# A macaron hybrid layer in fp32: the FFN's hidden activations transposed on VectorE in 32x32 blocks instead of on TensorE

## The chip, the cores and the metric

One core of a Trainium2 chip runs the whole layer. The metric is device time in microseconds of one execution, median of several runs. Engine names follow the profile: PE is TensorE's matmul, PEld its weight load, DVE is VectorE, ACT is ScalarE, POOL is GpSimd, SP is SyncE.

## The reference

One decoder layer on x of 256 rows by 2048 columns, all in float32: a half-step of SwiGLU FFN, a mixer with three groups of attention heads, and a second half-step of SwiGLU FFN. The change touches the two FFNs alone.

```python
def rms_norm(x, g):
    xf = x.astype(jnp.float32)
    y = xf * lax.rsqrt(jnp.mean(xf * xf, axis=-1, keepdims=True) + EPS)
    return (y * g.astype(jnp.float32)).astype(x.dtype)

def swiglu(x, w_gate, w_up, w_down):
    return (jax.nn.silu(x @ w_gate) * (x @ w_up)) @ w_down
...
        x = x + 0.5 * swiglu(rms_norm(x, ffn1_norm[l]), ffn1_gate[l], ffn1_up[l], ffn1_down[l])
        ...                                # the mixer: three groups of heads, then w_out
        x = x + 0.5 * swiglu(rms_norm(x, ffn2_norm[l]), ffn2_gate[l], ffn2_up[l], ffn2_down[l])
```

The gate and up weights are 2048 x 5632, the down weights 5632 x 2048.

## The kernel before

Every projection multiplies in three terms. A weight tile is split into a rounded part `hi` (ScalarE, L203) and the rest `lo` (VectorE, L204); the activations are split the same way (`split`, L207 to L209), and `mm_rows` (L241 to L248) adds hi times hi, hi times lo and lo times hi into one PSUM accumulator. The activations stand on the PE as weights of 128x128, and 512 columns of the layer's weights stream past them. `load_w` brings 256 rows by 512 columns at a time; I call this a block. It feeds 12 matmuls: two k tiles, two row tiles t, three terms. The raw tile has four buffers, `hi` and `lo` have three each, so the `hi` of a block can be written only when the PE has finished the block three before it.

`ffn` (L267) runs 11 rounds j of 512 hidden columns. A round is a gate projection (8 blocks, L292), SiLU on ScalarE into `g` (L298), an up projection (8 blocks, L300), and the product on VectorE (L302), which leaves h as 256 rows on partitions. The down projection needs h with hidden columns on partitions. So `transpose_h` (L273) has the PE transpose eight 128x128 squares into PSUM (L280), and splits them from there into the two halves of `hT` (L285, two calls of 512 elements per partition on each of ScalarE and VectorE). After the rounds, four down projections of 22 blocks each (L314 on) read `hT`.

What runs beside the projections is cut into stages by generators. `lanes.tick()` after each block (L263) advances them by one stage; `lanes.put` queues a task for one of two lanes that each own a PSUM buffer, `lanes.run` starts one without a lane. The engine order is then set by the framework's scheduler when the program is built. Within an engine, the order is fixed.

At the end of the last down projection (c = 3 of the second FFN), VectorE adds each row tile to x (L316), and `store` (L694) sends each as 128 x 512 to the output, t = 0 by SP's queue and t = 1 by ACT's.

Of the kernel before, what the change touches and what calls it, by code (L numbers as in the profile page):

```python
# [8 lines left out]
F32 = mybir.dt.float32  # L9
# [7 lines left out]
P = 128  # L17
D = 2048
NK = D // P
SEQ = 256  # L20
NT = SEQ // P
DFF = 5632
NF = DFF // P
# [3 lines left out]
KB = 2  # L27
# [53 lines left out]
def hybrid_layer(ctx, tc, x, mem, ffn1_norm, ffn1_gate, ffn1_up, ffn1_down, mix_norm, mem_norm,  # L81
# [3 lines left out]
    nc = tc.nc  # L85

    x, mem, out = x[0], mem[0], out[0]
    gate1, up1, down1 = ffn1_gate[0], ffn1_up[0], ffn1_down[0]
    gate2, up2, down2 = ffn2_gate[0], ffn2_up[0], ffn2_down[0]
# [11 lines left out]
    def psum(tag, name):  # L101

        return ps.tile([P, 2, 512], F32, tag=tag, bufs=2 if tag == "acc" else 1, name=name)

    lanes = Lanes()


    x_sb = cpool.tile([P, NT, D], F32, name="x_sb")
# [4 lines left out]
    for k0, nk in XCUT:  # L113
        cols = slice(k0 * P, (k0 + nk) * P)
        (nc.scalar if k0 else nc.sync).dma_start(x_sb[:, :, cols], xv[:, :, cols])

    ident = cpool.tile([P, P], F32, name="ident")
# [78 lines left out]
    def load_w(w, k0, nk, c0, width, name):  # L196
        raw = wpool.tile([P, KB, 512], F32, tag="raw", bufs=4, name=f"raw_{name}")
        hi = wpool.tile([P, KB, 512], F32R, tag="hi", bufs=3, name=f"hi_{name}")
        lo = wpool.tile([P, KB, 512], F32R, tag="lo", bufs=3, name=f"lo_{name}")
        r, h, l = (t[:, :nk, :width] for t in (raw, hi, lo))  # L200
        nc.sync.dma_start(
            r, w[k0 * P:(k0 + nk) * P, c0:c0 + width].rearrange("(k p) c -> p k c", p=P))
        nc.scalar.copy(h, r)  # L203
        nc.vector.tensor_tensor(out=l, in0=r, in1=h.bitcast(F32), op=ALU.subtract)  # L204
        return h, l

    def split(dst_hi, dst_lo, src):  # L207
        nc.scalar.copy(dst_hi, src)
        nc.vector.tensor_tensor(out=dst_lo, in0=src, in1=dst_hi.bitcast(F32), op=ALU.subtract)  # L209

    def transpose_chunk(xT, src, k0, nk, g0, name, pause=1):
# [16 lines left out]
            yield 1  # L228
        return stages

    def square_sums(ss, src, c):
        for t in range(NT):
            junk = small.tile([P, 512], F32, tag="junk", bufs=2, name="junk")
            nc.scalar.activation(junk, src[:, t, :], AF.Square, accum_out=ss[:, t, c:c + 1])
# [6 lines left out]
    def mm_rows(acc, aT, kt, wh, wl, first, last):  # L241

        w = wh.shape[-1]
        for t in range(NT):
            hi, lo = aT[:, kt, 0, t * P:(t + 1) * P], aT[:, kt, 1, t * P:(t + 1) * P]
            nc.tensor.matmul(acc[:, t, :w], hi, wh, start=first, stop=False)  # L246
            nc.tensor.matmul(acc[:, t, :w], hi, wl, start=False, stop=False)  # L247
            nc.tensor.matmul(acc[:, t, :w], lo, wh, start=False, stop=last)  # L248

    def project(acc, aT, w, c0, width, kts, nk_all, done, name, before=None):  # L250

        for k0, n in kts:
            k = k0
            while k < k0 + n:
                b = min(KB, k0 + n - k)
                if before:
                    before(k)
                wh, wl = load_w(w, k, b, c0, width, f"{name}_{k}")
                for j in range(b):
                    mm_rows(acc, aT, k + j, wh[:, j, :], wl[:, j, :], done == 0, done == nk_all - 1)  # L260
                    done += 1
                k += b
                lanes.tick()  # L263
        return done


    def ffn(xT, before, stats, wg, wu, wd, after, name):  # L267

        with tc.tile_pool(name=f"h_{name}", bufs=1, reuse_waits="tile") as hpool, \
                tc.tile_pool(name=f"ht_{name}", bufs=2, reuse_waits="tile") as htmp:  # L270
            hT = hpool.tile([P, NF, 2, SEQ], F32R, name=f"hT_{name}")

            def transpose_h(j, h):  # L273

                def stages(tag):
                    tp = psum(tag, f"th_{name}{j}")
                    tv = tp.rearrange("p a b -> p (a b)").rearrange("p (k s) -> p k s", k=4)
                    for k in range(4):
                        for t in range(NT):
                            nc.tensor.transpose(tv[:, k, t * P:(t + 1) * P], h[:, t, k * P:(k + 1) * P],  # L280
                                                ident)
                    yield 1
                    for b in range(2):
                        f = slice(4 * j + 2 * b, 4 * j + 2 * b + 2)
                        split(hT[:, f, 0, :], hT[:, f, 1, :], tv[:, 2 * b:2 * b + 2, :])  # L285
                    yield 1
                return stages

            rstd = None
            for j in range(DFF // 512):  # L290
                acc = psum("acc", f"g{name}{j}")
                project(acc, xT, wg, j * 512, 512, [(0, NK)], NK, 0, f"{name}g{j}",  # L292
                        None if j else before)
                if j == 0:
                    rstd = stats()
                g = htmp.tile([P, NT, 512], F32, tag="g", bufs=3, name=f"gs{name}{j}")
                for t in range(NT):
                    nc.scalar.activation(g[:, t, :], acc[:, t, :], AF.Silu, scale=rstd[:, t:t + 1])  # L298
                acc = psum("acc", f"u{name}{j}")
                project(acc, xT, wu, j * 512, 512, [(0, NK)], NK, 0, f"{name}u{j}")  # L300
                for t in range(NT):
                    nc.vector.scalar_tensor_tensor(out=g[:, t, :], in0=acc[:, t, :],  # L302
                                                   scalar=rstd[:, t:t + 1], in1=g[:, t, :],
                                                   op0=ALU.mult, op1=ALU.mult)
                lanes.put(f"hT{name}{j}", transpose_h(j, g))

            def before_d(k):
                if k >= NF - 4:
                    lanes.finish(f"hT{name}{DFF // 512 - 1}")

            for c in range(4):
                acc = psum("acc", f"d{name}{c}")
                project(acc, hT, wd, c * 512, 512, [(0, NF)], NF, 0, f"{name}d{c}", None if c else before_d)
                for t in range(NT):  # L314
                    xc = x_sb[:, t, c * 512:(c + 1) * 512]
                    nc.vector.scalar_tensor_tensor(out=xc, in0=acc[:, t, :], scalar=0.5, in1=xc,  # L316
                                                   op0=ALU.mult, op1=ALU.add)
                    after(c, t)

    def xchunk(c):  # L320
        return x_sb[:, :, c * 512:(c + 1) * 512]
# [6 lines left out]
    x0T = r1.tile([P, NK, 2, SEQ], F32R, tag="r1", name="x0T")  # L328
# [25 lines left out]
    def mem_stages_T(c):  # L354
        def stages(tag):
            raw = mem_raw(c)
            yield 3
            yield from transpose_chunk(lambda: memTs[0], lambda: raw, 4 * c, 4, G_MEM, f"mem{c}")(tag)
            square_sums(ssm, raw, c)
        return stages  # L360

    def after1(c, t):
        if t == 0:
            return
        if c == 0:
            memTs.append(r1.tile([P, NK, 2, SEQ], F32R, tag="r1", name="memT"))
        if c < 2:
            for i in (2 * c, 2 * c + 1):
                lanes.put(f"memT{i}", mem_stages_T(i), ("consts",))
        square_sums(ss1, xchunk(c), c)  # L370
# [2 lines left out]
        lanes.finish(*(f"ss0_{c}" for c in range(4)))  # L373
        return row_rstd(ss0, "x0")

    ffn(x0T, before0, stats0, gate1, up1, down1, after1, "a")
    memT = memTs[0]
    lanes.finish("memT3")

# [1 line left out]
    with tc.tile_pool(name="mix", bufs=1, reuse_waits="tile") as mx, \  # L381
# [39 lines left out]
        acc = psum("acc", "mk")  # L421
        project(acc, memT, w_mem_k, 0, 512, [(0, NK)], NK, 0, "mk")
        lanes.run("mk", heads_T(acc, 4, rm, 5, mkT, "mk"))
        acc = psum("acc", "mv")
# [8 lines left out]
        sv = slots[:, 30:32, :]  # L433
# [195 lines left out]
        acc = chunk(MEM_Q, 512, "mq")  # L629
# [4 lines left out]
        acc = chunk(FOX_F, 390, "sqa")  # L634
        for t in range(NT):
            nc.vector.scalar_tensor_tensor(out=z[:, t, :], in0=acc[:, t, 0:6], scalar=r1s[:, t:t + 1],
                                           in1=bias6, op0=ALU.mult, op1=ALU.add)
# [3 lines left out]
        acc = chunk(SWA_K, 512, "skv")  # L641
# [3 lines left out]
        acc = chunk(SWA_Q + 384, 384, "sqb")  # L645
# [4 lines left out]
        for half, (a, b) in (("a", (0, 3)), ("b", (3, 6))):  # L650
            for g, (c0, dst) in enumerate(((FOX_Q, fqT), (FOX_K, fkT))):
                name = f"f{'qk'[g]}{half}"
                acc = chunk(c0 + a * HD, 384, name)
# [6 lines left out]
        for half, a in (("a", 0), ("b", 384)):  # L660
            acc = chunk(FOX_V + a, 384, f"fv{half}")
# [14 lines left out]
        x2T = r1.tile([P, NK, 2, SEQ], F32R, tag="r1", name="x2T")  # L676
        for c in range(4):
            if c < 2:
                acc = accs[c]
                project(acc, mixT, w_out, c * 512, 512, late, 16, done[c], f"wo{c}l")  # L680
            else:
                acc = psum("acc", f"wo{c}")
                project(acc, mixT, w_out, c * 512, 512, [(0, 16)], 16, 0, f"wo{c}")
            xc = xchunk(c)
# [6 lines left out]

    ov = out.rearrange("(t p) d -> p t d", p=P)

    def store(c, t):  # L694
        cols = slice(c * 512, (c + 1) * 512)
        (nc.sync, nc.scalar)[t].dma_start(ov[:, t, cols], x_sb[:, t, cols])

    def stats2():
        lanes.finish("ss2_3")
        return row_rstd(ss2, "x2")  # L700

    ffn(x2T, lambda k: lanes.finish("bT3") if k == 12 else None, stats2, gate2, up2, down2, store, "b")


# [29 lines left out]
```

## Time and profile before

| what | value |
|---|---|
| median of 3 runs (lowest to highest) | 1833.58 us (1833.07 to 1834.23) |
| the profiled execution's own time | 1832.94 us |
| its span, first to last instruction | 1831.2 us |
| granted TensorE clock | 1.00 over the whole run |
| PE busy | 1818.1 us, 99% |
| DVE busy | 941.8 us, 51% |
| ACT busy | 846.1 us, 46% |
| the 88 transposes of h on PE in each FFN (L280) | 11.4 us busy |

Busy time counts an instruction from its start to its end. Instructions of one engine can overlap, so what one costs on the path is the distance from its start to the start of the next, which the timeline shows. Span and execution time differ by 1.7 us, which lies outside the instructions.

### The profile page before, as it was taken

How to read it: one execution, taken by the hardware profiler on the slowest of the kernel's cores; microseconds unless marked ns; L12 is line 12 of the kernel's file. 1: busy time of each engine (PE TensorE's matmuls, PEld its weight loads, DVE VectorE, ACT ScalarE, POOL GpSimd, SP SyncE). 2: the span in 40 equal slices, each digit the busy share in tenths (PEclk: the TensorE clock that was granted, in tenths of full speed). 3: DMA queues.
4: the chain of work that ended last, by engine and by line, in shares of the span. 5: the costliest groups of instructions: out<-in, count | busy, mean ns of one | idle time of the engine just before them, and what ended most of it. 6: DMA issues, size and time to landing. Idle time of an engine off the chain costs nothing.

```text
span 1831.2 us, 21875 instructions
## 1 busy us (share of the span) xinstructions
PE 1818.1 (99%) x8424; PEld 1532.2 (84%) x8424; DVE 941.8 (51%) x1127; ACT 846.1 (46%) x1148; POOL 11.6 (1%) x31
## 2 busy tenths in 40 slices
PE   8999999999999999999999999999999999999998
PEld 6888888888888888888999888888888888888887
DVE  5454545455545554645666455455545454544443
ACT  6444444444445444557666454444444444433332
POOL 2000000000000000000000000000000000000000
PEclk9999999999999999999999999999999999999999
DMA  7666666666666566565666556666666666666663
GB/s 235 191 190 189 190 190 188 192 189 190 190 190 206 188 216 193 167 178 156 181 156 183 171 185 193 186 193 188 192 184 190 189 189 190 191 193 203 205 207 127
DMA packets 182696, 344.55 MB, mean 188 GB/s; under 512 B 11130, under 2 KB 28096, under 8 KB 182464
## 3 DMA queue, kind: packets, MB, share of 16 engines
q1 hardware_dynamic: 180368, 339.04, 62.0%
q10 hardware_dynamic: 1696, 2.89, 0.5%
q8 instruction: 66, 1.08, 0.3%
q0 software_dynamic: 528, 1.22, 0.2%
q14 instruction: 38, 0.31, 0.0%
HBM read 341.01 MB, written 2.11 MB: 187 GB/s over the span
## 4 chain that ended last, share of the span: by engine, by line
PE 99%; DMA 0%; ACT 0%; DVE 0%; issue 0%; DVEq 0%; ACTq 0%
PE ga L246 4%; PE ga L248 4%; PE ga L247 4%; PE ua L246 4%; PE da L248 4%; PE gb L248 4%; PE db L248 4%; PE gb L247 4%; PE gb L246 4%; PE da L247 4%; PE ub L247 4%; PE ua L248 4%; PE da L246 4%; PE ua L247 4%; PE ub L248 4%; PE ub L246 4%
## 5 line engine op out<-in xcount | busy, mean ns | idle before, releaser
L204 DVE TENSOR_TENSOR lo_bu<-raw_bu,hi_bu 128x1024 fp32r<-128x1024 f32 x88 | 107.8, 1226 | 131.5 <-ACT hi_bu L203 131.5
L204 DVE TENSOR_TENSOR lo_au<-raw_au,hi_au 128x1024 fp32r<-128x1024 f32 x88 | 107.8, 1225 | 130.0 <-ACT hi_au L203 130.0
L204 DVE TENSOR_TENSOR lo_bd<-raw_bd,hi_bd 128x1024 fp32r<-128x1024 f32 x88 | 107.8, 1225 | 123.9 <-ACT hi_bd L203 123.9
L204 DVE TENSOR_TENSOR lo_ad<-raw_ad,hi_ad 128x1024 fp32r<-128x1024 f32 x88 | 107.8, 1225 | 116.7 <-ACT hi_ad L203 116.7
L203 ACT CAST hi_bd<-raw_bd 128x1024 fp32r<-128x1024 f32 x88 | 92.8, 1055 | 145.0 <-PE db L248 139.8
L204 DVE TENSOR_TENSOR lo_ag<-raw_ag,hi_ag 128x1024 fp32r<-128x1024 f32 x88 | 107.9, 1226 | 99.2 <-ACT hi_ag L203 99.2
L204 DVE TENSOR_TENSOR lo_bg<-raw_bg,hi_bg 128x1024 fp32r<-128x1024 f32 x88 | 107.7, 1224 | 99.1 <-ACT hi_bg L203 99.1
L203 ACT CAST hi_ad<-raw_ad 128x1024 fp32r<-128x1024 f32 x88 | 92.7, 1053 | 129.1 <-PE da L248 104.7
L203 ACT CAST hi_bg<-raw_bg 128x1024 fp32r<-128x1024 f32 x88 | 92.7, 1054 | 127.2 <-PE gb L248 68.3
L203 ACT CAST hi_ag<-raw_ag 128x1024 fp32r<-128x1024 f32 x88 | 92.8, 1054 | 121.3 <-PE ga L248 66.7
L203 ACT CAST hi_bu<-raw_bu 128x1024 fp32r<-128x1024 f32 x88 | 92.7, 1054 | 115.5 <-PE ub L248 79.0
L203 ACT CAST hi_au<-raw_au 128x1024 fp32r<-128x1024 f32 x88 | 92.7, 1054 | 115.3 <-PE ua L248 79.4
L246 PE MATMUL ga<-hi_ag,x0T 128*128 128x512 f32 x352 | 138.5, 393 | 0.0
L246 PE MATMUL gb<-hi_bg,x2T 128*128 128x512 f32 x352 | 137.9, 392 | 0.0
L246 PE MATMUL da<-hi_ad,hT_a 128*128 128x512 f32 x352 | 137.4, 390 | 0.0
L248 PE MATMUL ga<-hi_ag,x0T 128*128 128x512 f32 x352 | 137.4, 390 | 0.0
L247 PE MATMUL ga<-lo_ag,x0T 128*128 128x512 f32 x352 | 137.2, 390 | 0.0
L248 PE MATMUL gb<-hi_bg,x2T 128*128 128x512 f32 x352 | 137.1, 389 | 0.0
L247 PE MATMUL da<-lo_ad,hT_a 128*128 128x512 f32 x352 | 137.0, 389 | 0.0
L246 PE MATMUL ua<-hi_au,x0T 128*128 128x512 f32 x352 | 137.0, 389 | 0.0
L246 PE MATMUL db<-hi_bd,hT_b 128*128 128x512 f32 x352 | 137.0, 389 | 0.0
L248 PE MATMUL da<-hi_ad,hT_a 128*128 128x512 f32 x352 | 137.0, 389 | 0.0
(459 smaller groups left out, 3948.3 us busy)
## 6 DMA issues: line engine op xcount, KB each, us to landing
raw_ag<-in_ffn_gate_dram SPq DMA_DIRECT2D x88, 512.0 KB, 4.5
raw_au<-in_ffn_up_dram SPq DMA_DIRECT2D x88, 512.0 KB, 3.7
raw_ad<-in_ffn_down_dram SPq DMA_DIRECT2D x88, 512.0 KB, 4.1
raw_bg<-in_ffn_gate_dram SPq DMA_DIRECT2D x88, 512.0 KB, 4.2
raw_bu<-in_ffn_up_dram SPq DMA_DIRECT2D x88, 512.0 KB, 3.7
raw_bd<-in_ffn_down_dram SPq DMA_DIRECT2D x88, 512.0 KB, 4.4
raw_wo<-in_w_out_dram SPq DMA_DIRECT2D x16, 512.0 KB, 3.7
raw_mk<-in_w_mem_k_dram SPq DMA_DIRECT2D x8, 512.0 KB, 3.7
```

The source lines that it names most:

```text
L203: nc.scalar.copy(h, r)
L204: nc.vector.tensor_tensor(out=l, in0=r, in1=h.bitcast(F32), op=ALU.subtract)
L246: nc.tensor.matmul(acc[:, t, :w], hi, wh, start=first, stop=False)
L247: nc.tensor.matmul(acc[:, t, :w], hi, wl, start=False, stop=False)
L248: nc.tensor.matmul(acc[:, t, :w], lo, wh, start=False, stop=last)
```

## The change

`quad_transposes` is new: VectorE transposes 32x32 blocks. An instruction reads 32 partitions (group a of four) and writes 32 partitions (group b), eight blocks at a time, which are 256 elements per partition. Sixteen of them turn the 256 x 512 tile `g` into `raw`, 128 partitions by 4 by 256 in SBUF. They come in four stages of four. Then two stages split `raw` into `hT`. The task no longer needs a lane's PSUM buffer, and goes by `lanes.run`. `g` has two buffers instead of three, `raw` has one.

The end of the last down projection is reordered as well: `project_end` takes the last block apart, so that all six matmuls of t = 0 come before the six of t = 1. The second row tile is then added and stored in two halves of 256 columns.

```diff
+    def quad_transposes(dst, src):
+        sv = src.rearrange("p t (k b s) -> p b t k s", b=4, s=32)
+        dv = dst.rearrange("p k (t a s) -> p a t k s", t=NT, s=32)
+        for a in range(4):
+            for b in range(4):
+                nc.vector.transpose(out=dv[32 * b:32 * b + 32, a], in_=sv[32 * a:32 * a + 32, b])
+            yield 1
...
+    def project_end(acc, aT, w, c0, k0, n, name, landed):
+        tiles = []
+        for k in range(k0, k0 + n, KB):
+            wh, wl = load_w(w, k, KB, c0, 512, f"{name}_{k}")
+            tiles += [(wh[:, j, :], wl[:, j, :]) for j in range(KB)]
+        for t in range(NT):
+            for j, (wh, wl) in enumerate(tiles):
+                hi, lo = (aT[:, k0 + j, i, t * P:(t + 1) * P] for i in range(2))
+                nc.tensor.matmul(acc[:, t, :], hi, wh, start=False, stop=False)
+                nc.tensor.matmul(acc[:, t, :], hi, wl, start=False, stop=False)
+                nc.tensor.matmul(acc[:, t, :], lo, wh, start=False, stop=j == n - 1)
+            for c, width in ((0, 256), (256, 256)) if t else ((0, 512),):
+                landed(t, c, width)
+        lanes.tick()
...
             def transpose_h(j, h):
-                def stages(tag):
-                    tp = psum(tag, f"th_{name}{j}")
-                    tv = tp.rearrange("p a b -> p (a b)").rearrange("p (k s) -> p k s", k=4)
-                    for k in range(4):
-                        for t in range(NT):
-                            nc.tensor.transpose(tv[:, k, t * P:(t + 1) * P], h[:, t, k * P:(k + 1) * P],
-                                                ident)
+                raw = htmp.tile([P, 4, SEQ], F32, tag="raw", bufs=1, name=f"hr_{name}{j}")
+                yield from quad_transposes(raw, h)
+                for b in range(2):
+                    f = slice(4 * j + 2 * b, 4 * j + 2 * b + 2)
+                    split(hT[:, f, 0, :], hT[:, f, 1, :], raw[:, 2 * b:2 * b + 2, :])
                     yield 1
-                    for b in range(2):
-                        f = slice(4 * j + 2 * b, 4 * j + 2 * b + 2)
-                        split(hT[:, f, 0, :], hT[:, f, 1, :], tv[:, 2 * b:2 * b + 2, :])
-                    yield 1
-                return stages
...
-                g = htmp.tile([P, NT, 512], F32, tag="g", bufs=3, name=f"gs{name}{j}")
+                g = htmp.tile([P, NT, 512], F32, tag="g", bufs=2, name=f"gs{name}{j}")
...
-                lanes.put(f"hT{name}{j}", transpose_h(j, g))
+                lanes.run(f"hT{name}{j}", transpose_h(j, g))
...
+                ending = 2 if last and c == 3 else 0
+                project(acc, hT, wd, c * 512, 512, [(0, NF - ending)], NF, 0, f"{name}d{c}",
+                        None if c else before_d)
+                if ending:
+                    project_end(acc, hT, wd, c * 512, NF - ending, ending, f"{name}d{c}", landed)
...
+    def store(c, t, c0, width):
+        cols = slice(c * 512 + c0, c * 512 + c0 + width)
+        (nc.sync, nc.scalar)[t ^ (c0 > 0)].dma_start(ov[:, t, cols], x_sb[:, t, cols])
```

VectorE's order at the start of round j = 1 of the first FFN, before. `gsa0` is the h of round 0; `lo_ag1_4` is the `lo` of the gate block that begins at k = 4, which is the third block of the round; `th_a0` is h transposed in PSUM.

```order
L302 SCALAR_TENSOR_TENSOR gsa0_398<-ua0_401,y_x0_384,gsa0_398 128x512 x2
L204 TENSOR_TENSOR lo_ag1_4_605<-raw_ag1_4_603,hi_ag1_4_604 128x1024
L204 TENSOR_TENSOR lo_ag1_6_623<-raw_ag1_6_621,hi_ag1_6_622 128x1024
L209 TENSOR_TENSOR hT_a_115<-th_a0_572,hT_a_115 128x2x256 x2
L204 TENSOR_TENSOR lo_ag1_8_641<-raw_ag1_8_639,hi_ag1_8_640 128x1024
L204 TENSOR_TENSOR lo_ag1_10_659<-raw_ag1_10_657,hi_ag1_10_658 128x1024
L204 TENSOR_TENSOR lo_ag1_12_677<-raw_ag1_12_675,hi_ag1_12_676 128x1024
```

The same place on VectorE in the changed kernel; `hr_a0` is the new tile `raw`:

```order
L321 SCALAR_TENSOR_TENSOR gsa0_398<-ua0_401,y_x0_384,gsa0_398 128x512 x2
L204 TENSOR_TENSOR lo_ag1_4_601<-raw_ag1_4_599,hi_ag1_4_600 128x1024
L237 STREAM_TRANSPOSE hr_a0_572<-gsa0_398 32x2x4x32 x12
L204 TENSOR_TENSOR lo_ag1_6_623<-raw_ag1_6_621,hi_ag1_6_622 128x1024
L237 STREAM_TRANSPOSE hr_a0_572<-gsa0_398 32x2x4x32 x4
L204 TENSOR_TENSOR lo_ag1_8_645<-raw_ag1_8_643,hi_ag1_8_644 128x1024
L209 TENSOR_TENSOR hT_a_115<-hr_a0_572,hT_a_115 128x2x256
L204 TENSOR_TENSOR lo_ag1_10_665<-raw_ag1_10_663,hi_ag1_10_664 128x1024
L209 TENSOR_TENSOR hT_a_115<-hr_a0_572,hT_a_115 128x2x256
L204 TENSOR_TENSOR lo_ag1_12_685<-raw_ag1_12_683,hi_ag1_12_684 128x1024
```

Twelve of the sixteen transposes stand in one piece ahead of the fourth block's `lo`, and four ahead of the fifth's. All 22 rounds have this order; behind the last round of an FFN the blocks are those of the down projection.

PE's order at the same place, before (the last matmul of the round's first block, the transposes of h, the first matmuls of the second block). In the changed kernel the eight transposes are gone and nothing else moves here.

```order
L247 MATMUL ga1_553<-lo_ag1_0_556,x0T_108 128x512
L248 MATMUL ga1_553<-hi_ag1_0_555,x0T_108 128x512
L280 MATMUL th_a0_572<-ident_84,gsa0_398 128x128 x8
L246 MATMUL ga1_553<-hi_ag1_2_582,x0T_108 128x512
L247 MATMUL ga1_553<-lo_ag1_2_583,x0T_108 128x512
```

## Rows read from the trace of the kernel before

**Rows 1.** Busy time by engine, and the chain that ended last by engine

```profile
PE 1818.1 (99%) x8424; PEld 1532.2 (84%) x8424; DVE 941.8 (51%) x1127; ACT 846.1 (46%) x1148; POOL 11.6 (1%) x31
...
PE 99%; DMA 0%; ACT 0%; DVE 0%; issue 0%; DVEq 0%; ACTq 0%
```

**Rows 2.** PE's transposes of h, first FFN: count, busy us, mean ns, idle before

```profile
L280 PE MATMUL th_a<-ident,gsa 128*128 128x128 f32 x88 | 11.4, 272 | 0.0
```

**Rows 3.** Timeline of PE where a round starts: start us, us, instruction

```profile
323.75 0.39 PE L246 MATMUL ga<-hi_ag,x0T 128*128 128x512 f32 x1
323.98 0.39 PE L247 MATMUL ga<-lo_ag,x0T 128*128 128x512 f32 x1
...
326.48 1.03 PE L280 MATMUL th_a<-ident,gsa 128*128 128x128 f32 x8
327.27 0.48 PE L246 MATMUL ga<-hi_ag,x0T 128*128 128x512 f32 x1
327.58 0.40 PE L247 MATMUL ga<-lo_ag,x0T 128*128 128x512 f32 x1
```

**Rows 4.** Timeline of DVE over the same round, to the next round's start

```profile
314.16 1.23 DVE L204 TENSOR_TENSOR lo_au<-raw_au,hi_au 128x1024 fp32r<-128x1024 f32 x1 [1.50 <-ACT hi_au L203]
316.88 1.23 DVE L204 TENSOR_TENSOR lo_au<-raw_au,hi_au 128x1024 fp32r<-128x1024 f32 x1 [1.49 <-ACT hi_au L203]
...
323.95 1.41 DVE L302 SCALAR_TENSOR_TENSOR gsa<-ua,y_x,gsa 128x512 f32<-128x512 f32 x2 [0.41 <-PE ua L248]
325.28 1.22 DVE L204 TENSOR_TENSOR lo_ag<-raw_ag,hi_ag 128x1024 fp32r<-128x1024 f32 x1
327.75 1.23 DVE L204 TENSOR_TENSOR lo_ag<-raw_ag,hi_ag 128x1024 fp32r<-128x1024 f32 x1 [1.26 <-ACT hi_ag L203]
328.90 0.68 DVE L209 TENSOR_TENSOR hT_a<-th_a,hT_a 128x512 fp32r<-128x512 f32 x1
...
368.37 1.41 DVE L302 SCALAR_TENSOR_TENSOR gsa<-ua,y_x,gsa 128x512 f32<-128x512 f32 x2 [0.41 <-PE ua L248]
```

**Rows 5.** Timeline of ACT there

```profile
326.68 1.05 ACT L203 CAST hi_ag<-raw_ag 128x1024 fp32r<-128x1024 f32 x1 [1.67 <-PE ga L248]
327.63 0.58 ACT L208 CAST hT_a<-th_a 128x512 fp32r<-128x512 f32 x1
```

**Rows 6.** Timeline of DVE in the mixer: instructions that follow each other without a wait

```profile
886.61 0.42 DVE L522 TENSOR_REDUCE nm_w<-ss_w 128x2 f32<-128x256 f32 x1
886.95 0.16 DVE L185 TENSOR_SCALAR t_sqb<-v_sqb 128x8 int32<-128x8 int32 x1
...
895.60 0.55 DVE L468 TENSOR_TENSOR nck_all<-nck_all,cmask 128x384 f32<-128x384 f32 x1
896.06 0.17 DVE L459 RECIPROCAL ri_w<-sm_w 128x4 f32<-128x4 f32 x1
```

**Rows 7.** Groups of DVE by shape: 1024, 768 and 256 elements per partition

```profile
L204 DVE TENSOR_TENSOR lo_mq<-raw_mq,hi_mq 128x1024 fp32r<-128x1024 f32 x8 | 9.8, 1225 | 12.8 <-ACT hi_mq L203 12.8
...
L204 DVE TENSOR_TENSOR lo_fkb<-raw_fkb,hi_fkb 128x768 fp32r<-128x768 f32 x8 | 7.7, 957 | 4.2 <-ACT hi_fkb L203 4.2
...
L225 DVE SCALAR_TENSOR_TENSOR x0T<-tp_x,gT,x0T 128x256 fp32r<-128x256 f32 x16 | 7.2, 478 | 0.4 <-ACT x0T L224 0.4
...
L462 DVE TENSOR_SCALAR ss_m<-ss_m,ri_m 128x256 f32<-128x256 f32 x8 | 2.4, 349 | 0.1
```

**Rows 8.** One round by engine: stretch, its us, busy us (count), clock, DMA share, GB/s

```profile
323.76:368.18 44.42, 44.42 (x202) 36.87 (x201) 22.21 (x20) 19.09 (x20) 0.00 (x0) 1.00 0.66 190
```

**Rows 9.** DMA issues: size of each, median us to landing

```profile
raw_ag<-in_ffn_gate_dram SPq DMA_DIRECT2D x88, 512.0 KB, 4.5
```

**Rows 10.** Timeline of DVE and ACT's queue at the end

```profile
1826.05 1.29 DVE L316 SCALAR_TENSOR_TENSOR x_sb<-db,x_sb 128x512 f32<-128x512 f32 x2 [5.85 <-PE db L248]
...
1827.37 0.34 ACTq L696 DMA_DIRECT2D out_dram<-x_sb  x1
```

**Rows 11.** DMA issues of the last 12 us: the second store

```profile
out_dram<-x_sb ACTq DMA_DIRECT2D x1, 256.0 KB, 2.6
```

More of the change, by code (lines that the diff above doesn't have):

```diff
@@ L264, in project, with ffn @@
         return done
-    def ffn(xT, before, stats, wg, wu, wd, after, name):
+    def project_end(acc, aT, w, c0, k0, n, name, landed):
[12 more added lines that the diff above has]
+        lanes.tick()
+    def ffn(xT, before, stats, wg, wu, wd, after, last, name):
         with tc.tile_pool(name=f"h_{name}", bufs=1, reuse_waits="tile") as hpool, \
@@ L312, in ffn, with landed @@
                 acc = psum("acc", f"d{name}{c}")
[L313 to L316, printed above, removed]
+                def landed(t, c0, width):
+                    xc = x_sb[:, t, c * 512 + c0:c * 512 + c0 + width]
+                    nc.vector.scalar_tensor_tensor(out=xc, in0=acc[:, t, c0:c0 + width], scalar=0.5, in1=xc,
                                                    op0=ALU.mult, op1=ALU.add)
-                    after(c, t)
+                    after(c, t, c0, width)
+                ending = 2 if last and c == 3 else 0
[3 more added lines that the diff above has]
+                    project_end(acc, hT, wd, c * 512, NF - ending, ending, f"{name}d{c}", landed)
+                else:
+                    for t in range(NT):
+                        landed(t, 0, 512)
     def xchunk(c):
@@ L360, in mem_stages_T, with after1 @@
         return stages
-    def after1(c, t):
+    def after1(c, t, c0, width):
         if t == 0:
@@ L374, in stats0 @@
         return row_rstd(ss0, "x0")
-    ffn(x0T, before0, stats0, gate1, up1, down1, after1, "a")
+    ffn(x0T, before0, stats0, gate1, up1, down1, after1, False, "a")
     memT = memTs[0]
@@ L692, in hybrid_layer @@
     ov = out.rearrange("(t p) d -> p t d", p=P)
-    def store(c, t):
-        cols = slice(c * 512, (c + 1) * 512)
-        (nc.sync, nc.scalar)[t].dma_start(ov[:, t, cols], x_sb[:, t, cols])
+    def store(c, t, c0, width):
+        cols = slice(c * 512 + c0, c * 512 + c0 + width)
+        (nc.sync, nc.scalar)[t ^ (c0 > 0)].dma_start(ov[:, t, cols], x_sb[:, t, cols])
     def stats2():
@@ L700, in stats2 @@
         return row_rstd(ss2, "x2")
-    ffn(x2T, lambda k: lanes.finish("bT3") if k == 12 else None, stats2, gate2, up2, down2, store, "b")
+    ffn(x2T, lambda k: lanes.finish("bT3") if k == 12 else None, stats2, gate2, up2, down2, store, True, "b")
 _INS = ["x", "mem", "ffn1_norm", "ffn1_gate", "ffn1_up", "ffn1_down", "mix_norm", "mem_norm", "w_in",
```

## The prediction

> **What bounds the kernel now.** I read the busy times first, then the chain that ended last, then the timeline around one round. The first two agree: PE is busy for 1818.1 of 1831.2 us, and 99% of the chain is PE [rows 1]. So time leaves this kernel only where PE has less to do, and comes back only where PE starts to wait. DVE (51%) and ACT (46%) have room on average. In one round DVE is busy 22.21 of 44.42 us [rows 8]. An average doesn't say whether the room lies where it is needed, so the rest is about one place.
>
> The timeline shows the rhythm. PE starts a matmul about every 0.227 us: 12 of them from 323.75 to 326.48, which is one block, 2.72 us [rows 3]; DVE's `lo` comes at the same step, 314.16 to 316.88 [rows 4]. Between a round's first and second block stand the eight transposes. They are not hidden: matmuls before and behind them follow without idle time, and the group of 88 in each FFN shows none [rows 2, 3].
>
> **What is removed.** Their durations, 272 ns each [rows 2], overlap, so I take the path cost from the round. From one product on DVE to the next is 368.37 - 323.95 = 44.42 us [rows 4]. A round holds 16 blocks, 16 x 2.72 = 43.52 us. The transposes cost 0.90 us. Directly on PE: from 326.48 to 327.58 there pass 1.10 us for the eight and one matmul, less 0.23 for that one is 0.87 [rows 3]. I use 0.90. There are 176 transposes, 22 rounds: 22 x 0.90 = 19.8 us, at most.
>
> **What is added on DVE, and who waits.** Sixteen transposes per round, each 256 elements on 32 partitions. Behind them on DVE are queued the `lo` parts of the round's fourth and fifth block, and PE waits for those in its second matmul of each block. Call c the distance from one transpose's start to the next.
>
> The block starts on PE, without the old transposes: 323.75, 326.48, 329.20, 331.92 (fourth), 334.64 (fifth). Second matmuls come 0.23 later: 332.15 and 334.87.
>
> DVE starts the third block's `lo` at 325.28 [rows 4]. An instruction of that size lets the next one start 1.15 us after it (327.75 to 328.90, rows 4), so the transposes begin at 326.43. Then:
>
> - The fourth `lo` ends at 326.43 + 12c + 1.23 = 327.66 + 12c. It must be there by 332.15. With some 0.04 us for the signal (an ACT cast that ends at 327.73 lets DVE start at 327.75, rows 4, 5), c may be 0.37.
> - The fifth ends at 326.43 + 12c + 1.15 + 4c + 1.23 = 328.81 + 16c, due 334.87. With the signal c may again be 0.37 to 0.38.
> - Above that, PE stalls in each round for S, the larger of 12c - 4.45 and 16c - 6.02 us.
>
> The inputs are no obstacle: the fourth block's `hi` is cast from 326.68 to 327.73, while the transposes run [rows 5]. The first transpose needs the product of 323.95, done by 325.36 [rows 4].
>
> **How large c is.** No transpose on DVE is in the trace, so I bound it. The cheapest row of 256 elements is TENSOR_SCALAR with 0.349 us [rows 7]; if 0.08 of that is covered by the next, as below, 0.27. The dearest is the SCALAR_TENSOR_TENSOR from PSUM, 0.478 with no overlap [rows 7]. Between them stand instructions that take one element per step: 256 more elements cost 1225 - 957 = 268 ns, 1.05 ns per element [rows 7]. A TENSOR_REDUCE over 256 takes 0.42, but the next instruction starts 0.34 after it; a TENSOR_TENSOR of 384 lets the next start after 0.46, which is 0.33 for 256 [rows 6]. I take 0.34 as base, since a transpose also streams its elements once. A lane's first result lies 31 columns away in the source; if reading those first shows in full, it adds 32 x 1.05 ns = 0.03, an estimate. So c = 0.37, right at the edge: I put S at 0.05 us, 22 x 0.05 = 1.1 us in all. At c = 0.34 S is nothing, but PE can't gain more than 19.8. Toward zero cost, then, the gain is capped; toward 0.478, S is 16 x 0.478 - 6.02 = 1.63 us and the change loses.
>
> [...]
>
> **Other edits.** The two splits per round now read SBUF. DVE's keeps its element count (0.68 us, rows 4), and ACT's took 0.58 [rows 5]; a few hundredths more would fall into ACT's idle half [rows 8]. DVE's first split waits for ACT's, which waits for the sixteenth transpose, at 326.43 + 1.15 + 16 x 0.37 = 333.5; the cast ends about 334.1, and DVE reaches its split at about 334.7, after the fifth `lo`. So no bubble, and the sixth `lo`, behind the split (0.6) and 1.2 long, ends about 336.5, due 337.6. A late `lo` frees its raw tile late: the fourth's, freed at 332.1, is filled by 336.6 at 4.5 us [rows 9], and ACT wants it after 337.4. Cover of 0.8 us; if a landing took 5.5 us, the difference would add to S. One buffer less for `g` and one for `raw` cost nothing: each is read out within five blocks of sixteen. SP's loads keep their order, and both store queues only change the last three stores.
>
> The end: before, PE's last matmul is followed by two additions of 512, the second store goes out at 1827.37 [rows 10]. Now the first is added while PE works on t = 1. Two halves remain. Two additions of 512 took 1.29 [rows 10]; 256 elements less in each are 2 x 0.27 = 0.54 us less, at 1.05 ns [rows 7]. The last stores are half as large; the last one took 2.6 us to land [rows 11], and I let that give another 0.2 (between 0 and half of it). Together 0.7.
>
> **The sum.** The profiled execution took 1832.94 us: -19.8 + 1.1 - 0.7 gives 1813.5. The median lies 0.64 above it, so 1814.2; I say 1814.
>
> **Rivals.**
>
> A, the fixed part is not covered. If a transpose holds DVE until it has drained, c is 0.42, the TENSOR_REDUCE's duration [rows 6]. For it: no row shows whether this instruction overlaps with its like. Against it: four kinds of instructions in rows 4 and 6 all let the next start early. S = 16 x 0.42 - 6.02 = 0.70, 15.4 us: 1833.6 - 19.8 - 0.7 + 15.4 = 1828.5. [...]
>
> B, DVE becomes what PE waits for, at the fifth block of every round. The price of a transpose decides: from S = 0.93, that is c = 0.434, the change loses. At 0.478 [rows 7] S is 1.63, 35.8 us: 1848.9. If each element took two steps, c = 0.34 + 0.27 = 0.61 and S = 3.74: 1895. For it: twelve stand in one piece, and the limit of 0.37 leaves little above 0.34; a four-level pattern on 32 partitions has no neighbour in the trace. Against it: 1.05 ns per element in every row that streams f32 once.
>
> C, c between 0.385 and 0.41: S from 0.17 to 0.54 us, 1817 to 1825, a part of the gain lost in the same wait.
>
> **How the numbers follow.** Forecast (c up to 0.385, S up to 0.2, 1811.5 to 1818): 0.55. C: 0.13. A and its neighbourhood (c 0.41 to 0.445, 1825 to 1838): 0.13. B: 0.19. A measurement of this kernel can tell 0.2% from no change, 3.7 us. Faster by more than that is the forecast, C and a third of A: 0.72. Within it, half of A: 0.07. Slower, B and the rest of A: 0.21. No time below 1811.5 has a mechanism: 20.5 us off 1833.6 is 1813.1, and 1.6 us stand for what rounding leaves in 22 x 0.90 and for the last stores. The range goes up into B, to 1845 (c = 0.467), which leaves about 0.17 out.
>
> **What would show it.** Right: L280 gone from PE, a round of 43.5 us, DVE transposes 0.42 or so long that start every 0.34 to 0.37 us, PE's idle time before its `lo` matmuls near zero, three additions at the end, of 512, 256 and 256. Wrong: PE waiting for `lo_ag`, `lo_bg` from DVE at the fourth or fifth block, 22 times, 0.5 us or more each; or a round that is still 44.4 us although PE no longer transposes.

## The result, and the profile after

The changed kernel takes 1846.31 us (median of 4 runs, 1845.64 to 1847.72) against 1833.5 us before: the ratio is 1.007, 95% interval 1.0057 to 1.0082. It is slower by 12.8 us. The forecast was 1814 us, and 1845 the upper end of its range.

The page's busy times and its chain by engine, after (answers to [rows 1]):

```profile
PE 1812.8 (98%) x8248; PEld 1510.8 (82%) x8248; DVE 1087.3 (59%) x1480; ACT 846.0 (46%) x1148; POOL 11.6 (1%) x31
...
PE 83%; DVE 12%; issue 3%; DMA 2%; ACT 1%; ACTq 0%; DVEq 0%; POOLq 0%
```

PE has its 176 transposes less, and VectorE now has 12% of the chain, where it had nothing. The groups of the new instruction by shape (count, busy us, mean ns, idle before), and what PE waited for (us in total, times, longest):

```profile
L237 DVE STREAM_TRANSPOSE hr_a<-gsa 32x256 f32<-32x256 f32 x176 | 76.7, 436 | 2.5
L237 DVE STREAM_TRANSPOSE hr_b<-gsb 32x256 f32<-32x256 f32 x176 | 76.7, 436 | 2.5
```

```profile
PE ga L256 <- DVE lo_ag L204: 7.9, 10, 0.8
PE gb L256 <- DVE lo_bg L204: 7.9, 10, 0.8
...
PE da L256 <- DVE lo_ad L204: 1.3, 2, 0.8
PE db L256 <- DVE lo_bd L204: 0.8, 1, 0.8
PE db L285 <- DVE x_sb L335: 0.8, 1, 0.8
```

The waits are where the prediction put them: 22 of the 23 shown before a `lo` matmul, 0.79 us each, come once per round (in the last round of an FFN at the down projection, `da` or `db`). The second one of `da`, 0.48 us at 654.27, stands far behind the transposes, where VectorE and ScalarE prepare the mixer's `memT`. The view lists waits above 0.15 us only, so the shorter ones at the fifth block aren't in it. VectorE's timeline over one round (answers to [rows 4]):

```profile
326.87 1.41 DVE L321 SCALAR_TENSOR_TENSOR gsa<-ua,y_x,gsa 128x512 f32<-128x512 f32 x2 [0.41 <-PE ua L257]
328.19 1.22 DVE L204 TENSOR_TENSOR lo_ag<-raw_ag,hi_ag 128x1024 fp32r<-128x1024 f32 x1
329.32 5.37 DVE L237 STREAM_TRANSPOSE hr_a<-gsa 32x256 f32<-32x256 f32 x12
334.73 1.23 DVE L204 TENSOR_TENSOR lo_ag<-raw_ag,hi_ag 128x1024 fp32r<-128x1024 f32 x1
335.98 1.79 DVE L237 STREAM_TRANSPOSE hr_a<-gsa 32x256 f32<-32x256 f32 x4
337.81 1.23 DVE L204 TENSOR_TENSOR lo_ag<-raw_ag,hi_ag 128x1024 fp32r<-128x1024 f32 x1
...
371.84 1.41 DVE L321 SCALAR_TENSOR_TENSOR gsa<-ua,y_x,gsa 128x512 f32<-128x512 f32 x2 [0.41 <-PE ua L257]
```

A round is 371.84 - 326.87 = 44.97 us, where it was 44.42 and would be 43.52 without waits. Twelve transposes fill 5.37 us: from start to start c = (5.37 - 0.436) / 11 = 0.449 us, more than the 0.436 that one lasts. None lets the next begin early: in the trace each starts 0.013 to 0.015 us after the end of the one before. PE over the fourth and fifth block (answers to [rows 3]):

```profile
334.82 0.39 PE L255 MATMUL ga<-hi_ag,x0T 128*128 128x512 f32 x1
336.01 0.50 PE L256 MATMUL ga<-lo_ag,x0T 128*128 128x512 f32 x1 [0.79 <-DVE lo_ag L204]
336.34 0.39 PE L257 MATMUL ga<-hi_ag,x0T 128*128 128x512 f32 x1
...
338.64 0.39 PE L255 MATMUL ga<-hi_ag,x0T 128*128 128x512 f32 x1
339.09 0.50 PE L256 MATMUL ga<-lo_ag,x0T 128*128 128x512 f32 x1
339.43 0.39 PE L257 MATMUL ga<-hi_ag,x0T 128*128 128x512 f32 x1
```

The second matmul follows 1.19 us behind the first instead of 0.23 (0.96 lost), and in the fifth block 0.45 behind it (0.22 lost). The matmul after each takes 0.33 and 0.34 to come instead of 0.23, another 0.21. Together 1.39 of the 1.45 us that the round lost against 43.52; several of the matmuls right behind come up to 0.01 us late each. So 0.90 was won per round and 1.45 paid: 22 x 0.55 = 12.1 us.

The end of the program on PE and VectorE (answers to [rows 10]):

```profile
1836.31 0.39 PE L285 MATMUL db<-hi_bd,hT_b 128*128 128x512 f32 x1
...
1837.44 0.39 PE L287 MATMUL db<-hi_bd,hT_b 128*128 128x512 f32 x1
1837.87 0.69 DVE L335 SCALAR_TENSOR_TENSOR x_sb<-db,x_sb 128x512 f32<-128x512 f32 x1 [4.49 <-PE db L287]
1838.61 0.50 PE L285 MATMUL db<-hi_bd,hT_b 128*128 128x512 f32 x1 [0.78 <-DVE x_sb L335]
```

The first matmul of t = 1 waits until the addition of t = 0 is done. From the last block's first matmul to the end of the span there pass 1844.4 - 1836.31 = 8.09 us. In the kernel before, where that matmul started 11 x 0.227 ahead of the last one at 1825.62, it was 1831.2 - 1823.13 = 8.07 us. The end brought nothing. So 0.7 of the 12.8 us are not accounted for by the rounds.

### The profile page after: what moved, and what is told of

It is laid out like the page before. It is cut to its first block, busy times and chain, and to the rows that moved or that the text cites. A ratio compares the mean times of both kernels' runs of the same rounds, so it can differ in the third digit from the quotient of the medians.

```text
span 1844.4 us, 21899 instructions
## 1 busy us (share of the span) xinstructions
PE 1812.8 (98%) x8248; PEld 1510.8 (82%) x8248; DVE 1087.3 (59%) x1480; ACT 846.0 (46%) x1148; POOL 11.6 (1%) x31
## 4 chain that ended last, share of the span: by engine, by line
PE 83%; DVE 12%; issue 3%; DMA 2%; ACT 1%; ACTq 0%; DVEq 0%; POOLq 0%
PE ua L255 4%; PE ub L257 4%; PE ua L256 4%; PE ua L257 4%; PE ub L255 4%; PE ub L256 4%; PE db L256 4%; PE db L257 4%; PE db L255 4%; DVE hr_a L237 4%; PE da L256 4%; PE da L257 4%; PE da L255 4%; DVE hr_b L237 4%; PE ga L256 3%
## 5 line engine op out<-in xcount | busy, mean ns | idle before, releaser
L256 PE MATMUL gb<-lo_bg,x2T 128*128 128x512 f32 x352 | 139.3, 396 | 8.5 <-DVE lo_bg L204 7.9
L255 PE MATMUL ua<-hi_au,x0T 128*128 128x512 f32 x352 | 137.0, 389 | 0.0
L257 PE MATMUL ua<-hi_au,x0T 128*128 128x512 f32 x352 | 136.9, 389 | 0.0
L256 PE MATMUL ua<-lo_au,x0T 128*128 128x512 f32 x352 | 136.9, 389 | 0.0
```

## The experiments

The first theory was that c alone had been mis-sized, and that nothing else in the change costs time. The rivals were a cost of the transposes wherever they stand, and different reasons for c.

**One transpose per stage** (e1_one_per_stage). The work is the same, but it is spread over more blocks.

```diff
                 nc.vector.transpose(out=dv[32 * b:32 * b + 32, a], in_=sv[32 * a:32 * a + 32, b])
-            yield 1
+                yield 1
```

> The changed kernel with one transpose per stage in place of four; DVE then has 4, 5, 5 and 2 transposes ahead of the lo parts of the fourth to seventh block, in place of 12 and 4. Theory (each transpose holds VectorE for 0.45 us, and PE loses only what the fourth and fifth lo come too late): with 4 x 0.45 the fourth lo ends at 326.43 + 1.80 + 1.23 = 329.5, due 332.15, the fifth at about 333.0, due 334.87; no stall, a round of 43.5 us, 1833.5 - 19.8 = 1813.7 us, PE's waits for lo_ag and lo_bg gone. Rival (the sum of VectorE's work, or its traffic in SBUF, slows the round wherever it stands): still near 1846, a round of 44.9 or more.

Measured: 1814.04 us, ratio 0.9892 (0.9877 to 0.9907). VectorE's timeline:

```profile
320.92 1.22 DVE L204 TENSOR_TENSOR lo_ag<-raw_ag,hi_ag 128x1024 fp32r<-128x1024 f32 x1
322.05 1.77 DVE L237 STREAM_TRANSPOSE hr_a<-gsa 32x256 f32<-32x256 f32 x4
323.85 1.23 DVE L204 TENSOR_TENSOR lo_ag<-raw_ag,hi_ag 128x1024 fp32r<-128x1024 f32 x1
325.11 2.23 DVE L237 STREAM_TRANSPOSE hr_a<-gsa 32x256 f32<-32x256 f32 x5
327.37 1.23 DVE L204 TENSOR_TENSOR lo_ag<-raw_ag,hi_ag 128x1024 fp32r<-128x1024 f32 x1
```

The transposes cost as much as in the changed kernel (436 ns, c = 0.45), yet all 20 rounds within the FFNs are 43.52 us long, and no wait of PE for `lo_ag` or `lo_bg` is left. The rival falls: VectorE's additional work costs PE nothing if `lo` is in time. Of the prediction's 19.8 us, 1833.5 - 1814.0 = 19.5 were there to be had, and were lost by where the transposes stood.

**The end alone** (e2_end_alone). The changed kernel with `transpose_h` and its buffers as before; `project_end` and the split store stay.

```diff
...                                        # transpose_h and the buffers of g as before
-                lanes.run(f"hT{name}{j}", transpose_h(j, g))
+                lanes.put(f"hT{name}{j}", transpose_h(j, g))
```

> Transposes of h on PE as before; only the reordered last block and its three additions and stores are kept. Theory (the first addition and PE's matmuls of t = 1 use one PSUM tile, so PE waits for the addition, 0.94 us, and the shorter end gives back 1.06): 0.1 us faster than before, 1833.4, PE's 0.78 us wait for x_sb there again. Rival (the end is worth the 0.7 us of the prediction, and the wait in the changed kernel came from elsewhere): 1832.8 without that wait.

Measured: 1834.01 us, ratio 1.0001 (0.9991 to 1.001), PE's wait for x_sb 0.8 us as in the changed kernel; from the last block's first matmul to the end 1832.6 - 1824.61 = 7.99 us. No change that can be told from none; the 0.7 us of the prediction are excluded by the trace, not by the interval.

**Copies in the same pattern** (e3_copies). Each transpose is a plain copy between the same groups of partitions.

```diff
-                nc.vector.transpose(out=dv[32 * b:32 * b + 32, a], in_=sv[32 * a:32 * a + 32, b])
+                nc.vector.tensor_copy(dv[32 * b:32 * b + 32, a], sv[32 * a:32 * a + 32, b])
```

> The changed kernel with each of the 352 transposes replaced by a plain VectorE copy between the same 32-partition patterns, in the same places; h is therefore not transposed within its blocks. Theory (transposing itself costs 0.436 us and holds the engine to its end): a copy takes 0.35 us or less and lets the next start 0.27 us or less after it, 12 x 0.27 = 3.2 us, no stall, 1813.7 us. Rival (the pattern on 32 partitions with runs of 32 elements costs it): copies that start every 0.45 us, 1846 us.

Measured: 1814.14 us, ratio 0.9892 (0.9872 to 0.9912), rounds of 43.52. The timeline of VectorE:

```profile
320.77 3.55 DVE L237 COPY hr_a<-gsa 32x256 f32<-32x256 f32 x12
324.36 1.23 DVE L204 TENSOR_TENSOR lo_ag<-raw_ag,hi_ag 128x1024 fp32r<-128x1024 f32 x1
325.61 1.19 DVE L237 COPY hr_a<-gsa 32x256 f32<-32x256 f32 x4
```

The time came out as the theory said, but its reason is damaged. A copy lasts 0.284 us and the next starts (3.55 - 0.284) / 11 = 0.297 us after it: copies don't overlap either, and the `lo` behind them starts at 324.36, after their end at 324.32. So it isn't transposing that holds the engine to its end. The time came out because a copy is also 0.15 us shorter, which leaves its step below the limit of 0.37.

**Half as many elements, twice as many instructions** (e4_halves).

```diff
-                nc.vector.transpose(out=dv[32 * b:32 * b + 32, a], in_=sv[32 * a:32 * a + 32, b])
+                for t in range(NT):
+                    nc.vector.transpose(out=dv[32 * b:32 * b + 32, a, t], in_=sv[32 * a:32 * a + 32, b, t])
```

> The changed kernel with each transpose cut in two of 128 elements, one for each row tile: 32 per round, ahead of the third, fourth and fifth block's lo 16, 8 and 8. Theory (a fixed part of 0.18 us that is not covered, and 1.05 ns per element): 0.31 us from start to start; the fifth lo ends 325.28 + 32 x 0.31 + 3 x 1.25, due 334.87, so a stall of 4.1 us per round and 1833.5 - 19.8 + 90 = 1904 us. Rival (a small fixed part and 1.4 ns per element, a price of each 32x32 block): 0.26 us, a stall of 2.5 us, 1869 us. If all of it is per element: 0.225 us, 1846.

Measured: 1870.68 us, ratio 1.02 (1.018 to 1.0221), 46.08 us per round. That is the rival's number, 1869. But the chain (start, us, what) shows another pattern than a price per element:

```profile
337.29 0.50 DVE hr_a L238 x2
337.79 0.01 issue
337.80 0.50 DVE hr_a L238 x2
...
339.82 0.01 issue
339.84 0.50 DVE hr_a L238 x2
```

The halves go in pairs of 0.51 us. The two of a pair read and write the same groups of partitions, and from one pair to the next a group changes. Two of 128 that never overlap would take two durations of the mean 0.281 and two gaps of 0.014, 0.590. So one start of two comes some 0.08 us early. Instruction by instruction, the trace shows which one: the second half starts 0.236 us behind the first, 0.066 before that one ends; the next pair starts 0.273 behind, 0.014 after the end. The rule that this suggests: an instruction that reads or writes another group of 32 partitions than the one before it starts only when that one has ended. Going from one group to another within an instruction isn't what holds it: 12 of the 16 pairs do that, and their second halves start early all the same.

**The same transposes, each within its own group** (e5_home_group). One index of the destination differs, and only every fourth changes its group.

```diff
-                nc.vector.transpose(out=dv[32 * b:32 * b + 32, a], in_=sv[32 * a:32 * a + 32, b])
+                nc.vector.transpose(out=dv[32 * a:32 * a + 32, b], in_=sv[32 * a:32 * a + 32, b])
```

> The changed kernel with the same 16 transposes per round in the same places, but each writes into the partition group that it reads (32a instead of 32b), so that only every fourth changes its group; the blocks stay in their own partition group, so h is not placed as the reference wants it. Theory (an instruction on VectorE that reads or writes another partition group than the one before it starts only when that one has ended; one that doesn't starts some 0.08 us earlier): nine of the twelve start 0.355 us apart, the fourth lo ends near 332.2, due 332.15, the fifth near 335.0, due 334.87; a round of 43.6 to 43.8 us, 1815 to 1820 us. Rival (a transpose always holds the engine to its end): starts 0.45 us apart throughout, a round of 44.97, 1846 us.

Measured: 1815.4 us, ratio 0.9898 (0.9883 to 0.9913), rounds of 43.57. VectorE's timeline:

```profile
320.77 1.22 DVE L204 TENSOR_TENSOR lo_ag<-raw_ag,hi_ag 128x1024 fp32r<-128x1024 f32 x1
321.90 4.26 DVE L237 STREAM_TRANSPOSE hr_a<-gsa 32x256 f32<-32x256 f32 x12
326.19 1.23 DVE L204 TENSOR_TENSOR lo_ag<-raw_ag,hi_ag 128x1024 fp32r<-128x1024 f32 x1
327.45 1.43 DVE L237 STREAM_TRANSPOSE hr_a<-gsa 32x256 f32<-32x256 f32 x4
328.91 1.23 DVE L204 TENSOR_TENSOR lo_ag<-raw_ag,hi_ag 128x1024 fp32r<-128x1024 f32 x1
```

The same number of the same instructions in the same places take 4.26 us where they took 5.37: (4.26 - 0.394) / 11 = 0.35 us from start to start on average (0.394 is their median duration). Instruction by instruction in the trace, the nine that stay in their group start 0.34 us behind the one before (0.326 to 0.370), the prediction's number, and 0.066 before that one ends. The two that change the group start 0.405 behind, 0.013 after the end; they last 0.435 and the others 0.392. The order of instructions is the same. Nor is it a semaphore: of the changed kernel's sixteen transposes in this round, thirteen wait for none. This settles what c is made of.

That a change of the group that is read suffices can be seen in the timeline of e1_one_per_stage above. The `lo` ahead of each piece reads and writes from partition 0 on. The second piece begins with a transpose that reads group 1 and writes group 0, so only the group that is read changes: it begins at 325.11, after that `lo` ended at 325.08. The first piece begins with one that reads and writes group 0: it begins at 322.05, before its `lo` ended at 322.14.

**Spread, and two PSUM tiles at the end** (e6_spread_two_tiles), which is the better version that the runs point to. `Pair` is a small class that gives each row tile its own tile.

```diff
...
                 acc = psum("acc", f"d{name}{c}")
+                if last and c == 3:
+                    acc = Pair(acc, psum("l0", f"d{name}{c}t"))
```

> One transpose per stage as in e1_one_per_stage, and in the last down projection the two row tiles accumulate in two PSUM tiles, so that the first addition and PE's last six matmuls share none. Theory: rounds of 43.5 us stay, PE's wait of 0.78 us for x_sb goes with the slow matmul behind it, 1814.0 - 1.0 = 1813.0 us. Rival (the addition would then be late anyway, or the second tile brings a wait of its own): 1814.0 with another wait at the end.

Measured: 1812.25 us, ratio 0.9883 (0.9866 to 0.9899), rounds of 43.52. The end on PE and VectorE:

```profile
1803.19 0.39 PE L294 MATMUL db<-hi_bd,hT_b 128*128 128x512 f32 x1
...
1804.55 0.39 PE L294 MATMUL db3t<-hi_bd,hT_b 128*128 128x512 f32 x1
1804.75 0.69 DVE L346 SCALAR_TENSOR_TENSOR x_sb<-db,x_sb 128x512 f32<-128x512 f32 x1 [4.49 <-PE db L296]
1804.78 0.39 PE L295 MATMUL db3t<-lo_bd,hT_b 128*128 128x512 f32 x1
```

PE no longer waits for the addition, and from the last block's first matmul to the end there pass 1810.2 - 1803.19 = 7.01 us, 1.08 less than in the changed kernel. So the wait was the shared PSUM tile. Against e1 the run times can't tell 1 us, since the two intervals overlap; the trace can. This version is faster than both kernels.

**Four `hi` and `lo` buffers** (e7_four_buffers). To make room, the mixer's temporaries and two scratch tiles of the sums of squares have one buffer instead of two.

```diff
-        hi = wpool.tile([P, KB, 512], F32R, tag="hi", bufs=3, name=f"hi_{name}")
-        lo = wpool.tile([P, KB, 512], F32R, tag="lo", bufs=3, name=f"lo_{name}")
+        hi = wpool.tile([P, KB, 512], F32R, tag="hi", bufs=4, name=f"hi_{name}")
+        lo = wpool.tile([P, KB, 512], F32R, tag="lo", bufs=4, name=f"lo_{name}")
...                                        # the mixer's and the scratch tiles' buffers
```

> The changed kernel with four hi and lo buffers instead of three; the mixer's temporaries have one buffer instead of two to make room, so only the FFN rounds are compared. All 16 transposes then stand in one piece ahead of the fifth lo, and the fourth is done before them. Theory (PE waits only because the lo parts queue behind the transposes with too little in stock): the fifth lo ends at 323.95 + 1.33 + 1.13 + 16 x 0.4485 + 0.04 + 1.23 = 334.86, due 334.87; a round of 43.5 to 43.7 us with the transposes still 0.45 us apart. Rival (the transposes themselves disturb PE or the loads): a round near 44.9.

Measured: 43.73 us per round (1818.11 us in all, ratio 0.9913, 0.9893 to 0.9933). VectorE:

```profile
322.32 1.22 DVE L204 TENSOR_TENSOR lo_ag<-raw_ag,hi_ag 128x1024 fp32r<-128x1024 f32 x1
323.45 7.18 DVE L237 STREAM_TRANSPOSE hr_a<-gsa 32x256 f32<-32x256 f32 x16
330.66 1.22 DVE L204 TENSOR_TENSOR lo_ag<-raw_ag,hi_ag 128x1024 fp32r<-128x1024 f32 x1
```

All sixteen stand in one piece, 0.45 us apart, and the round still loses only 0.21 us, since one more `lo` is in stock. PE's second matmul of the fifth block comes 0.27 us behind the first instead of 0.23, and the next one 0.34 behind it, so the slow matmul came even with a wait of 0.04 us. The rival's 44.9 is excluded: where `lo` is in time, the transposes cost PE nothing.

## Why the prediction was wrong

- **What is removed, 0.90 us per round: right.** Rounds without waits are 43.52 us long in e1, e3 and e6.
- **Who waits, where, and from which c: right.** PE waits at the second matmul of the fourth and fifth block. With the measured c = 0.449, 12c - 4.45 gives 0.94 us for the first wait (measured 0.96), and 16c - 6.02 gives 1.16 for both (measured 1.18). The signal from VectorE to PE, put at 0.04 us from rows that show 0.02, measured 0.05 (`lo` ends at 335.96, PE starts at 336.01).
- **How large c is: wrong, and this decided the sign.** The step was "I take 0.34 as base", with the early start seen in [rows 4, 6]. Those rows are all instructions on partitions from 0 on, so none of them changes its group; the new one changes it each time. Without the early start c is the duration, 0.436, and a gap of 0.013, together 0.449; where the group stays the same the starts are 0.34 apart (e5), which is the base without the 0.03 that the prediction added to it, and in e4 one start of two comes 0.066 before an end. The premise that a transpose streams its elements once held: 128 elements more took 0.133 us more, 1.04 ns each (0.236 + 0.066 = 0.302 to 0.435 us where the group changes, 0.273 - 0.014 = 0.259 to 0.392 where it stays; e4, e5). The duration itself was foreseen well, "0.42 or so". The point from which the change loses stood in the text, 0.434.
- **What a wait costs PE: a term was missing.** With the measured c the prediction's own sum would give S = 1.16, 25.6 us, and 1833.6 - 19.8 - 0.7 + 25.6 = 1838.7 us: a loss, but inside its range. A stall was priced at the wait alone. The runs showed 0.21 us more per round for the matmuls behind the two waits, 4.6 us in all. With the 0.7 of the end that makes 1844.0; the remaining 2.3 us up to 1846.3 are placed in part only (0.06 us per round, 1.3 us, in the matmuls that follow).
- **The rivals.** The mechanism was A's, no cover between transposes, and the price went over B's point: 0.449 against 0.42 in A. Sixteen times 0.03 us are 0.46 us per round, 10 us in all, the slow matmuls another 0.21 us per round, 4.6 us, and the end 0.7. That is 15.5 of the 17.8 us from 1828.5 to 1846.3, and leaves the same 2.3.
- **The end: wrong, 0.7 us against nothing.** I saw the addition beside PE's work on t = 1 and didn't ask what PE waits for there. Both use one PSUM tile, and the program orders a write into it behind the read (e2, e6).

## What to carry to other kernels

An engine that is half idle on average can still stop another, if work is put in one piece ahead of what that one needs next: 12 x 0.45 us in a queue that had 4.5 us of stock. The same work in smaller pieces was free. When a forecast hangs on a quantity that no row shows, and its breaking point lies within 0.06 us of the estimate, the rows taken as its neighbours must agree in what the new instruction does differently, here the partitions.

## What the runs showed of the hardware

- On VectorE, an instruction on 32 partitions started 0.013 to 0.015 us after the end of the one before it on 32 partitions if it read or wrote another partition group, for transposes and copies alike (0.449 and 0.297 us apart, at 0.436 and 0.284 us each). Transposes of 256 elements that stayed in their group started 0.34 us apart, 0.066 before the end of the one before (e5). Copies within a group were not run.
- After a wait, PE's next matmul came 0.33 to 0.34 us behind the one that had waited, instead of 0.23, with the granted clock at 1.00 over the run. Why is not shown.
